# Stationary values and 512-wide weight columns in the experts' second product, and a state-space layer without GpSimd

## The chip, the cores and the metric

The kernel runs on one core of a Trainium2 chip. The metric is the device time of one execution in microseconds; the time before is the median of three runs, 2701.28 us (2698.32 to 2701.37). The engines are TensorE (matmuls; PE, and PEld for its weight loads), VectorE (DVE), ScalarE (ACT), GpSimd (POOL) and SyncE (SP), whose queue issues most loads.

## The reference

A transformer of two parts on 256 positions of width 1024. The first part has a feed-forward layer, a mixer of two attentions, and another feed-forward layer. The second part has two layers. Each is a mixer (a state-space layer first, retention second), then a layer of 16384 experts (PEER), then a gated projection of a side input p. All in float32; the lines that matter here:

```python
seg = jnp.where(causal, cum[:, :, None] - cum[:, None, :], -jnp.inf)   # ssd_chunk_step
w = jnp.exp(seg) * cb[..., None] * dtc[:, None]
y = jnp.einsum('btsgr,bsgrp->btgrp', w, xc)
...
y = y.reshape(B, S, DI).astype(h.dtype) * jax.nn.silu(z)                # ssd_mixer
...
hid = jax.nn.gelu(jnp.einsum('tkd,td->tk', u[ib], xb), approximate=False)   # peer_ffn
return jnp.einsum('tk,tkd->td', (gb * hid).astype(xb.dtype), v[ib])
...
g = jax.nn.sigmoid(rms_norm_2(h, ple_norm[i]) @ ple_gate[i])            # second_block
h = h + g * (p[i] @ ple_proj[i])
```

## The kernel before

The residual x lies feature-major: 8 blocks (d) of 128 features by 256 positions. A float32 product is three matmuls (mm3): both operands are split into a high part (ah, wh) and a rest (al, wl), and the product of the two rests is left out. Weights come through one stream (class Stream) in units of 128 x 1024: SyncE loads w, ScalarE casts it to wh (L252), VectorE subtracts to get wl (L254; with pool_every = 4, as in the state-space layer, GpSimd takes every fourth). Three units are loaded ahead, two or three are split ahead.

The order on each engine is written by the framework's scheduler, which simulates the program with its own costs; code under high_priority is moved forward. Each engine then runs its queue strictly in order.

**Experts (peer).** All 16384 experts are computed for all positions. The first product gives G (two tiles G0 and G1, 64 blocks each), which the gates multiply. In the second product, the loop over e takes 128 units of 128 experts, in pairs; for each of 8 feature blocks d the 128 x 128 weights stand in TensorE and the 256 positions of the values (ah, al) move. The eight sums acc stay in four accumulator banks until the end. At the last pair each d is added to x (L1174) as soon as its sum is complete, and ready(d) calls prep: ScalarE makes ah, VectorE al, ScalarE the square, GpSimd adds the squares into sqa. Two 128-position halves are called t.

**Gated projection (ple).** It loads pT, splits it (ph, pl; L337 and L338), multiplies it with two units (the projection, 48 matmuls of 256 columns, copied to proj) and then multiplies the prepared x with eight units (the gate). The reduction of sqa over features is one matmul (L394). Its tiles lie in memory that the experts' pools have given up.

**State-space layer (ssd).** Per group of 8 heads: conv (cv, three steps of ca, ct) on 6 products, decays (e: cumulative sums plus mask on GpSimd, Exp on ScalarE), core (mt, e times mt, matmuls into po, y), gate (z, tanh, y; squares) and normed. Six of eight heads' e are multiplied on VectorE, two on GpSimd. Products are evacuated by VectorE through four banks. settle rescales x in eight blocks on ScalarE and GpSimd (scale_residual).

Of the kernel before, what the change touches and what calls it, by code (L numbers as in the profile page):

```python
# [21 lines left out]
FT = mybir.dt.float32  # L22
# [4 lines left out]
AF = mybir.ActivationFunctionType  # L27
OP = mybir.AluOpType
# [3 lines left out]
P = 128  # L32
S = 256
NT = S // P
D = 1024
KC = D // P
# [3 lines left out]
NEG = -1e30  # L40
# [4 lines left out]
PK, PH, PT = 128, 8, 16  # L45
# [48 lines left out]
def causal_constants():  # L94


    i = np.arange(P)
    low = np.where(i[None, :] <= i[:, None], 0.0, NEG)
    add = np.concatenate([low, np.zeros((P, P)), low], 1)
    up = np.where(i[None, :] >= i[:, None], 0.0, NEG)  # L100
    top = np.concatenate([up, np.zeros((P, P)), up], 1)
    return add.astype(np.float32), top.astype(np.float32)


# [200 lines left out]
class Program:  # L305
# [120 lines left out]
    def scale_residual(self, g, r, chunks):  # L426
        for c in chunks:
            x = self.x[:, c, :]
            self.nc.scalar.activation(x, x, AF.Identity, scale=self.vec(g, c))
            self.nc.gpsimd.tensor_tensor(x, x, r, OP.mult)  # L430

# [333 lines left out]
    def ssd(self, r, settle, ready):  # L767

        nc, ws = self.nc, self.ws
        with ExitStack() as ctx:  # L770
# [42 lines left out]
            def by_token():  # L813
                ps = self.bank("sc")
                for t in range(NT):
                    for j, k in enumerate((0, 2)):
                        o = (2 * t + j) * H
                        nc.tensor.transpose(ps[:, o:o + H], dt[:, k, t * P:(t + 1) * P], self.ident[:H, :H])
                ps = ps[:, :NT * 2 * H].rearrange("p (t j h) -> p t j h", t=NT, j=2)
                nc.vector.tensor_copy(tok[:, :, 0, :], ps[:, :, 0, :])  # L820
                nc.vector.tensor_scalar(tok[:, :, 1, :], ps[:, :, 1, :], -1.0, None, op0=OP.mult)


            def conv(ps, blk, dst):
# [12 lines left out]

            def decays(g, out):

                for i in range(0, G8, 2):  # L840
                    e = work.tile([P, 2, 384], FT, name="e", bufs=G8 // 2)
                    both = [P, 2, S]
                    nc.gpsimd.tensor_tensor(e[:, :, :S], cums[g][:, i:i + 2, :],
                                            mask[:, None, :S].to_broadcast(both), OP.add)
                    both = [P, 2, P]
                    nc.gpsimd.tensor_tensor(e[:, :, S:], cums[g][:, i:i + 2, P:],
                                            mask[:, None, S:].to_broadcast(both), OP.add)
                    for s in range(2):
                        h = G8 * g + i + s
                        for t, o in ((0, slice(0, S)), (1, slice(S, 384))):  # L850
                            nc.scalar.activation(e[:, s, o], e[:, s, o], AF.Exp, bias=tok[:, t, 1, h:h + 1])
                        out.append(e[:, s, :])
                    yield
                if g + 2 < SSD_G:
                    spread(g + 2)

            def core(g):
# [12 lines left out]
                nc.tensor.matmul(ps[:, :S], bc[:, 0, :P], bc[:, 1, :], start=True, stop=True)  # L870
                nc.tensor.matmul(ps[:, S:384], bc[:, 0, P:], bc[:, 1, P:], start=True, stop=True)
                mt = work.tile([P, 384], FT, name="mt")
                nc.scalar.copy(mt, ps[:, :384])
                yield
                ys[g] = y = work.tile([P, 4, S], FT, name="y")
                for j in range(4):
                    po = self.bank("po")
                    for s in range(2):
                        i = 2 * j + s
                        e = es[i]  # L880
                        (nc.gpsimd if i in (1, 5) else nc.vector).tensor_tensor(e, e, mt, OP.mult)
                        rows, c = slice(64 * s, 64 * s + 64), slice(64 * i, 64 * i + 64)
                        nc.tensor.matmul(po[rows, :S], xd[0][:, c], e[:, :S], start=True, stop=False,
                                         skip_group_check=True)
                        nc.tensor.matmul(po[rows, P:S], xd[1][:, c], e[:, S:], start=False, stop=True,
                                         skip_group_check=True)
                    nc.vector.scalar_tensor_tensor(y[:, j, :], xg[:, j, :], self.vec("ssd_d", 4 * g + j), po[:, :S],
                                                   op0=OP.mult, op1=OP.add)
                    yield

            def gate(ps, g, j):

                last = g == SSD_G - 1
                y = ys[g][:, j, :]
                z, t = work.tile([P, S], FT, name="z", bufs=3), work.tile([P, S], FT, name="zt", bufs=3)
                nc.vector.scalar_tensor_tensor(z, ps[:, :S], 0.5, r(), op0=OP.mult, op1=OP.mult)  # L896
                nc.scalar.activation(t, z, AF.Tanh)
                nc.gpsimd.tensor_tensor(y, y, z, OP.mult)
                nc.vector.scalar_tensor_tensor(y, t, 1.0, y, op0=OP.add, op1=OP.mult)
                self.square(y, j == 0, add=nc.vector if last else nc.gpsimd)  # L900
                if last and j == 2:
                    self.near_sqrt(y[:, 0:1])

            def normed(g):
# [157 lines left out]
    def peer(self, l, r, g, ready):  # L1062
        nc, ws = self.nc, self.ws
        with ExitStack() as ctx:
# [82 lines left out]
                nc.scalar.activation(G[b // (PK // 4)][:, 2 * b % (PK // 2):2 * b % (PK // 2) + 2, :],  # L1147
                                     ps.rearrange("p (a t) -> p a t", a=2), AF.Gelu)
            side.finish()
            acc = self.accumulators()  # L1150
            side = Side(gated(1, work))
            group = []
            for e in range(PK):
# [12 lines left out]
                    continue  # L1166
                if e == PK - 1:
                    self.new_parts()
                for d in (0, 2, 4, 6, 1, 3, 5, 7):
                    k = slice(d * P, (d + 1) * P)  # L1170
                    for i, (wh, wl), h, lo in group:
                        self.mm3(acc[d], wh[:, k], wl[:, k], h, lo, i == 0 and d % 2 == 0, i == PK - 1)
                    if e == PK - 1:
                        nc.vector.scalar_tensor_tensor(self.x[:, d, :], acc[d], 1.0 / GATE, self.x[:, d, :],  # L1174
                                                       op0=OP.mult, op1=OP.add)
                        ready(d)
                group = []
                side.run(1.2)

    def route(self, l, pool, qT, tabs):  # L1180

# [154 lines left out]
        self.ws.lend(stack.enter_context(self.tc.tile_pool(name="spare", bufs=n)), n, until)  # L1336
        return stack

    def accumulators(self):
        self.phase_banks()  # L1340
        four = [self.ps2_pool.tile([P, 2, S], FT, name=f"acc{i}") for i in range(4)]
        return [four[d // 2][:, d % 2, :] for d in range(KC)]

    def run(self):
        nc, tc = self.nc, self.tc
        with ExitStack() as ctx:
# [85 lines left out]
            for l in range(2):  # L1432
                if l == 0:
                    self.phase_banks(sc=2, po=2)
                    self.ws.pool_every = 4
                    self.ssd(r, settle(), before(f"ffn_norm_2{l}"))
                    more.close()
                    spare.close()
                    self.ws.pool_every = 0
                    self.ws.ahead = 2  # L1440
                else:
                    self.phase_banks(sc=1, po=1, pv=2)
                    self.retention(r, before(f"ffn_norm_2{l}"))
                    more.close()
                    spare.close()
# [55 lines left out]
```

## Time and profile before

| | |
|---|---|
| median of three runs | 2701.28 us |
| profiled execution | 2700.06 us |
| its span | 2698.2 us |
| mean granted TensorE clock | 0.991 of full |
| TensorE busy | 2641.6 us, 98% |
| VectorE, ScalarE, GpSimd busy | 2032.9, 1323.9, 313.9 us |

The span is the part of the execution that the trace covers. Matmuls overlap: one of 256 columns is shown 0.28 us long, but the next starts 0.12 us later, so the distance between starts is what counts. Busy time is the union of what an engine runs.

### The profile page before, as it was taken

The page shows a single profiled execution, that of the slowest core. Times are in us where ns is not written, and L with a number is a line of the kernel's source. Part 1 is how long each engine was busy: PE and PEld are TensorE (multiplying, and loading weights), DVE is VectorE, ACT ScalarE, POOL GpSimd, SP SyncE. Part 2 cuts the span into 40 slices and gives each one's busy share as a digit, 9 for nine tenths or more (in the row PEclk, how much of TensorE's full clock was granted, in tenths as well). Part 3 has the DMA queues.
Part 4 walks back from the last instruction along what each step waited for, and adds up shares of the span by engine and source line. Part 5 has one row for each costly group of instructions (what it writes and reads, how often), then busy time and mean ns, then how long its engine had stood idle before and what let it go on. Part 6 is the DMA issues. An engine that isn't in the chain of part 4 may idle for free. (4 is left out here: it accounts for less than half of the span.)

```text
span 2698.2 us, 55170 instructions
## 1 busy us (share of the span) xinstructions
PE 2641.6 (98%) x22838; PEld 2592.4 (96%) x22838; DVE 2032.9 (75%) x3439; ACT 1323.9 (49%) x1810; POOL 313.9 (12%) x303
## 2 busy tenths in 40 slices
PE   8999999988999999999999999999999999999998
PEld 8998899978899999999999999999999999999998
DVE  8656766699779998868875576667999886886556
ACT  6445654666454444343344455555544334434445
POOL 1000100365510220000000020010122000000002
PEclk9999999999999999999999999999999999999999
DMA  6664365553455655555556555555555555556653
GB/s 214 186 186 138 122 191 175 175 185 115 133 177 181 185 171 169 161 174 166 168 182 186 182 172 184 159 171 176 180 187 176 159 163 172 173 163 187 186 181 118
DMA packets 128060, 460.58 MB, mean 171 GB/s; under 512 B 14688, under 2 KB 15424, under 8 KB 127168
## 3 DMA queue, kind: packets, MB, share of 16 engines
q1 hardware_dynamic: 125984, 452.32, 54.0%
q0 software_dynamic: 1536, 4.20, 0.5%
q8 instruction: 179, 2.93, 0.4%
q14 instruction: 73, 0.60, 0.1%
q10 hardware_dynamic: 288, 0.53, 0.1%
HBM read 455.91 MB, written 1.08 MB: 169 GB/s over the span
## 5 line engine op out<-in xcount | busy, mean ns | idle before, releaser
L252 ACT CAST wh<-w 128x1024 fp32r<-128x1024 f32 x856 | 887.1, 1038 | 1207.8 <-PE mm L318 617.4
L254 DVE TENSOR_TENSOR wl<-w,wh 128x1024 fp32r<-128x1024 f32 x842 | 1037.6, 1234 | 457.9 <-ACT wh L252 452.6
L317 PE MATMUL mm<-ah,wh 128*128 128x256 f32 x3448 | 985.6, 286 | 19.9 <-DVE z L896 9.4
L319 PE MATMUL mm<-ah,wl 128*128 128x256 f32 x3448 | 981.6, 285 | 5.7 <-DVE wl L254 5.4
L318 PE MATMUL mm<-al,wh 128*128 128x256 f32 x3448 | 982.3, 285 | 0.1
L317 PEld LDWEIGHTS mm<-ah,wh 128*128 128x128 f32 x3448 | 663.5, 193 | 22.6 <-ACT wh L252 8.4
L319 PEld LDWEIGHTS mm<-ah,wl 128*128 128x128 f32 x3448 | 663.7, 193 | 10.6 <-DVE wl L254 8.8
L318 PEld LDWEIGHTS mm<-al,wh 128*128 128x128 f32 x3448 | 664.0, 193 | 1.1 <-issue 0.5
L317 PE MATMUL acc<-ah,wh 128*128 128x256 f32 x2048 | 580.1, 284 | 0.0
L318 PE MATMUL acc<-al,wh 128*128 128x256 f32 x2048 | 578.8, 283 | 0.0
L319 PE MATMUL acc<-ah,wl 128*128 128x256 f32 x2048 | 575.7, 283 | 0.0
L318 PEld LDWEIGHTS acc<-al,wh 128*128 128x128 f32 x2048 | 393.0, 192 | 0.0
L317 PEld LDWEIGHTS acc<-ah,wh 128*128 128x128 f32 x2048 | 392.5, 192 | 0.0
L319 PEld LDWEIGHTS acc<-ah,wl 128*128 128x128 f32 x2048 | 391.2, 192 | 0.0
L362 POOL TENSOR_TENSOR sqa<-sqa,sqt 128x256 f32<-128x256 f32 x91 | 91.0, 1000 | 1741.9 <-ACT sqt L361 1647.5
L1118 DVE TENSOR_TENSOR G<-mm,G 128x512 f32<-128x512 f32 x128 | 88.1, 689 | 71.7 <-PE mm L1114 71.0
L317 PE MATMUL mm<-hh,wh 128*128 128x256 f32 x352 | 99.0, 281 | 0.0
L318 PE MATMUL mm<-hl,wh 128*128 128x256 f32 x352 | 99.0, 281 | 0.0
L319 PE MATMUL mm<-hh,wl 128*128 128x256 f32 x352 | 99.0, 281 | 0.0
L1102 DVE TENSOR_TENSOR two<-iota,tabs 128x1024 f16<-128x1024 f16 x128 | 87.4, 683 | 0.0
L1114 PE MATMUL mm<-one,two 128*128 128x64 f16 x2048 | 81.9, 193 | 0.0
L338 DVE TENSOR_TENSOR al<-G,ah 128x1024 fp32r<-128x1024 f32 x64 | 78.0, 1218 | 0.7 <-ACT ah L337 0.7
(349 smaller groups left out, 3371.7 us busy)
## 6 DMA issues: line engine op xcount, KB each, us to landing
w<-in_peer_u_dram SPq DMA_DIRECT2D x256, 512.0 KB, 3.6
w<-in_peer_v_dram SPq DMA_DIRECT2D x256, 512.0 KB, 3.6
w<-in_ffn_gu_dram SPq DMA_DIRECT2D x88, 512.0 KB, 3.7
w<-in_ssd_in_dram SPq DMA_DIRECT2D x40, 512.0 KB, 3.6
w<-in_ffn_dn_dram SPq DMA_DIRECT2D x32, 512.0 KB, 3.6
w<-in_peer_q_dram SPq DMA_DIRECT2D x32, 512.0 KB, 3.7
w<-in_ssd_out_dram SPq DMA_DIRECT2D x16, 512.0 KB, 3.6
w<-in_ple_g_dram SPq DMA_DIRECT2D x16, 512.0 KB, 3.6
```

Of the source, the lines that this page charges most:

```text
L252: nc.scalar.copy(h[:, :n], w[:, :n])
L254: (nc.gpsimd if own else nc.vector).tensor_tensor(l[:, :n], w[:, :n], h[:, :n].bitcast(FT), OP.subtract)
L317: mm(ps, h, xh, start=start, stop=False, skip_group_check=True)
L318: mm(ps, h, xl, start=False, stop=False, skip_group_check=True)
L319: mm(ps, l, xh, start=False, stop=stop, skip_group_check=True)
L338: self.nc.vector.tensor_tensor(l, x, h.bitcast(FT), OP.subtract)
L362: (add or nc.gpsimd).tensor_tensor(self.sq[tag], self.sq[tag], t, OP.add)
L1102: nc.vector.tensor_tensor(two, keys.to_broadcast(every), tab[1].to_broadcast(every), OP.is_equal)
L1114: nc.tensor.matmul(ps[:, t, :], two[:, t // 2, :, t % 2], one[i][:, t // 2, :, t % 2], start=i == 0, stop=i == 1)
L1118: nc.vector.tensor_tensor(ga, ps.rearrange("p t e -> p e t"), ga, OP.mult)
```

## The change

Three things change.

1. In the experts' second product the values stand in TensorE (128 positions at a time) and 512 weight columns move. The four sums acc[t][k] are position-major, one bank each. At the end a new function, features, copies each to memory of G0 (ScalarE), transposes it with 16 matmuls per layer, adds the result to x two blocks at a time, and calls ready.
2. The state-space layer has no GpSimd work. The mask becomes a factor (1 or 0) and goes into mt on VectorE; e is exp(-relu(own - other)), all on ScalarE (four Relu and one Exp per pair of heads); e times mt is one VectorE instruction per pair; the gate is three VectorE instructions beside tanh; squares are added on VectorE; scale_residual is one VectorE instruction.
3. All weight subtractions are VectorE's there (pool_every = 0).

```diff
-    up = np.where(i[None, :] >= i[:, None], 0.0, NEG)
-    top = np.concatenate([up, np.zeros((P, P)), up], 1)
+    up = np.where(i[None, :] >= i[:, None], 1.0, 0.0)
+    top = np.concatenate([up, np.ones((P, P)), up], 1)
...
-            self.nc.scalar.activation(x, x, AF.Identity, scale=self.vec(g, c))
-            self.nc.gpsimd.tensor_tensor(x, x, r, OP.mult)
+            self.nc.vector.scalar_tensor_tensor(x, x, self.vec(g, c), r, op0=OP.mult, op1=OP.mult)
...
-                nc.vector.tensor_copy(tok[:, :, 0, :], ps[:, :, 0, :])
-                nc.vector.tensor_scalar(tok[:, :, 1, :], ps[:, :, 1, :], -1.0, None, op0=OP.mult)
+                nc.vector.tensor_copy(tok, ps)
...
             def decays(g, out):
...
                 for i in range(0, G8, 2):
...
-                    both = [P, 2, S]
-                    nc.gpsimd.tensor_tensor(e[:, :, :S], cums[g][:, i:i + 2, :],
-                                            mask[:, None, :S].to_broadcast(both), OP.add)
-                    both = [P, 2, P]
-                    nc.gpsimd.tensor_tensor(e[:, :, S:], cums[g][:, i:i + 2, P:],
-                                            mask[:, None, S:].to_broadcast(both), OP.add)
                     for s in range(2):
...
                         for t, o in ((0, slice(0, S)), (1, slice(S, 384))):
-                            nc.scalar.activation(e[:, s, o], e[:, s, o], AF.Exp, bias=tok[:, t, 1, h:h + 1])
-                        out.append(e[:, s, :])
+                            nc.scalar.activation(e[:, s, o], cums[g][:, i + s, t * P:], AF.Relu, scale=-1.0,
+                                                 bias=tok[:, t, 1, h:h + 1])
+                    nc.scalar.activation(e, e, AF.Exp, scale=-1.0)
+                    out.append(e)
...
-                nc.scalar.copy(mt, ps[:, :384])
+                nc.vector.tensor_tensor(mt, ps[:, :384], mask, OP.mult)
...
                 for j in range(4):
...
+                    e = es[j]
+                    nc.vector.tensor_tensor(e, e, mt[:, None, :].to_broadcast([P, 2, 384]), OP.mult)
                     for s in range(2):
...
-                        e = es[i]
-                        (nc.gpsimd if i in (1, 5) else nc.vector).tensor_tensor(e, e, mt, OP.mult)
...
-                        nc.tensor.matmul(po[rows, :S], xd[0][:, c], e[:, :S], start=True, stop=False,
+                        nc.tensor.matmul(po[rows, :S], xd[0][:, c], e[:, s, :S], start=True, stop=False,
...
-                        nc.tensor.matmul(po[rows, P:S], xd[1][:, c], e[:, S:], start=False, stop=True,
+                        nc.tensor.matmul(po[rows, P:S], xd[1][:, c], e[:, s, S:], start=False, stop=True,
...
             def gate(ps, g, j):
...
-                last = g == SSD_G - 1
...
                 z, t = work.tile([P, S], FT, name="z", bufs=3), work.tile([P, S], FT, name="zt", bufs=3)
...
                 nc.scalar.activation(t, z, AF.Tanh)
-                nc.gpsimd.tensor_tensor(y, y, z, OP.mult)
-                nc.vector.scalar_tensor_tensor(y, t, 1.0, y, op0=OP.add, op1=OP.mult)
-                self.square(y, j == 0, add=nc.vector if last else nc.gpsimd)
-                if last and j == 2:
+                nc.vector.scalar_tensor_tensor(z, t, 1.0, z, op0=OP.add, op1=OP.mult)
+                nc.vector.tensor_tensor(y, y, z, OP.mult)
+                self.square(y, j == 0, add=nc.vector)
+                if g == SSD_G - 1 and j == 2:
...
-            acc = self.accumulators()
+            self.phase_banks()
+            acc = [[self.ps2_pool.tile([P, 512], FT, name=f"acc{t}{k}") for k in range(2)] for t in range(NT)]
...
                 if e == PK - 1:
...
-                for d in (0, 2, 4, 6, 1, 3, 5, 7):
-                    k = slice(d * P, (d + 1) * P)
-                    for i, (wh, wl), h, lo in group:
-                        self.mm3(acc[d], wh[:, k], wl[:, k], h, lo, i == 0 and d % 2 == 0, i == PK - 1)
+                for k in range(2):
+                    w = slice(512 * k, 512 * k + 512)
+                    for t in range(NT):
+                        o = slice(t * P, (t + 1) * P)
+                        for i, (wh, wl), h, lo in group:
+                            self.mm3(acc[t][k], h[:, o], lo[:, o], wh[:, w], wl[:, w], i == 0, i == PK - 1)
                     if e == PK - 1:
-                        nc.vector.scalar_tensor_tensor(self.x[:, d, :], acc[d], 1.0 / GATE, self.x[:, d, :],
-                                                       op0=OP.mult, op1=OP.add)
-                        ready(d)
+                        self.features(acc, k, G[0], ready)
...
+    def features(self, acc, k, room, ready):
+        nc = self.nc
+        with self.tc.high_priority(offset=200):
+            y = [room[:, 4 * k + 2 * t:4 * k + 2 * t + 2, :].rearrange("p a b -> p (a b)") for t in range(NT)]
+            for t in range(NT):
+                nc.scalar.activation(y[t], acc[t][k], AF.Copy, scale=1.0 / GATE)
+            for i in range(0, 4, 2):
+                ps = self.bank().rearrange("p (a t) -> p a t", a=2)
+                for j in range(2):
+                    for t in range(NT):
+                        nc.tensor.transpose(ps[:, j, t * P:(t + 1) * P], y[t][:, (i + j) * P:(i + j + 1) * P], self.ident)
+                d = 4 * k + i
+                nc.vector.tensor_tensor(self.x[:, d:d + 2, :], self.x[:, d:d + 2, :], ps, OP.add)
+                for j in range(2):
+                    ready(d + j)
...
-                    self.ws.pool_every = 4
+                    self.ws.pool_every = 0
```

Where instructions move, engine by engine. First SyncE's queue around the load of pT, first of the two layers; before:

```order
L238 DMA w<-in_ssd_out_dram 128x1024 x16
L238 DMA w<-in_peer_q_dram 128x1024 x16
L238 DMA w<-in_peer_u_dram 128x1024 x128
L238 DMA w<-in_peer_v_dram 128x1024 x62
L1256 DMA pT<-in_pT_dram 128x512
L238 DMA w<-in_peer_v_dram 128x1024 x66
L238 DMA w<-in_ple_p_dram 128x1024 x2
```

after:

```order
L238 DMA w<-in_peer_u_dram 128x1024 x128
L238 DMA w<-in_peer_v_dram 128x1024 x128
L238 DMA w<-in_ple_p_dram 128x1024 x2
L238 DMA w<-in_ple_g_dram 128x1024 x4
L1269 DMA pT<-in_pT_dram 128x512
L238 DMA w<-in_ple_g_dram 128x1024 x4
L238 DMA w<-in_ret_qk_dram 128x1024 x4
```

The load of pT stood behind 62 of the 128 units of the second product; now it stands behind all of them, the projection's two and four of the gate's.

Second, TensorE at the end of the same product (ph, pl: the projection's operand; G: the memory that features borrows); before:

```order
L317 MATMUL acc_14786<-ah,wh 128x256
L318 MATMUL acc_14786<-al,wh 128x256
L319 MATMUL acc_14786<-ah,wl 128x256
L317 MATMUL mm<-ph,wh 128x256
L318 MATMUL mm<-pl,wh 128x256
L319 MATMUL mm<-ph,wl 128x256
L317 MATMUL mm<-ph,wh 128x256
L318 MATMUL mm<-pl,wh 128x256
L319 MATMUL mm<-ph,wl 128x256
L317 MATMUL mm<-ph,wh 128x256
L318 MATMUL mm<-pl,wh 128x256
```

after:

```order
L318 MATMUL acc_14748<-wl,ah 128x512
L319 MATMUL acc_14748<-wh,al 128x512
L317 MATMUL acc_14748<-wh,ah 128x512
L318 MATMUL acc_14748<-wl,ah 128x512
L319 MATMUL acc_14748<-wh,al 128x512
L1187 MATMUL mm<-ident,G_8837 128x128 x16
L317 MATMUL mm<-ph,wh 128x256 x4
L318 MATMUL mm<-pl,wh 128x256
```

The projection's matmuls stood between those of the last pair; now the 16 transposes follow the last product matmul, and the projection follows them. On VectorE, around pl; before:

```order
L254 TENSOR_TENSOR wl<-w,wh 128x1024
L1118 TENSOR_TENSOR G_12053<-mm,G_12053 128x64x8
L254 TENSOR_TENSOR wl<-w,wh 128x1024
L1118 TENSOR_TENSOR G_12053<-mm,G_12053 128x64x8
L338 TENSOR_TENSOR pl<-pT,ph 128x512
L254 TENSOR_TENSOR wl<-w,wh 128x1024 x2
L338 TENSOR_TENSOR al<-G_12053,ah 128x1024
L254 TENSOR_TENSOR wl<-w,wh 128x1024 x5
```

after:

```order
L338 TENSOR_TENSOR al<-G_12012,ah 128x1024
L254 TENSOR_TENSOR wl<-w,wh 128x1024 x8
L1189 TENSOR_TENSOR x<-x,mm 128x512 x4
L254 TENSOR_TENSOR wl<-w,wh 128x1024 x2
L349 SCALAR_TENSOR_TENSOR al<-x,vecs,ah 128x256 x8
L338 TENSOR_TENSOR pl<-pT,ph 128x512
L1280 COPY proj<-mm 128x512 x2
L254 TENSOR_TENSOR wl<-w,wh 128x1024
L1280 COPY proj<-mm 128x512 x2
L254 TENSOR_TENSOR wl<-w,wh 128x1024 x2
```

The subtraction pl stood among the gates' products in the middle of the stage; now it follows the four additions to x, two weight subtractions and eight al of the next stage.

Third, GpSimd in the state-space layer, a piece of its rows before:

```order
L843 TENSOR_TENSOR e<-cums,mask 128x2x256
L846 TENSOR_TENSOR e<-cums,mask 128x2x128
L254 TENSOR_TENSOR wl<-w,wh 128x1024
L843 TENSOR_TENSOR e<-cums,mask 128x2x256
L846 TENSOR_TENSOR e<-cums,mask 128x2x128
L898 TENSOR_TENSOR y<-y,z 128x256
L843 TENSOR_TENSOR e<-cums,mask 128x2x256
L846 TENSOR_TENSOR e<-cums,mask 128x2x128
L898 TENSOR_TENSOR y<-y,z 128x256
L843 TENSOR_TENSOR e<-cums,mask 128x2x256
L846 TENSOR_TENSOR e<-cums,mask 128x2x128
L898 TENSOR_TENSOR y<-y,z 128x256
```

and all that it has between the stages on either side now:

```order
L362 TENSOR_TENSOR sqb<-sqb,sqt 128x256
L362 TENSOR_TENSOR sqa<-sqa,sqt 128x256
L362 TENSOR_TENSOR sqb<-sqb,sqt 128x256
L1205 DMA keys<-in_peer_k_dram 128x256
L362 TENSOR_TENSOR sqa<-sqa,sqt 128x256 x7
L1205 DMA keys<-in_peer_k_dram 128x256 x7
```

None of its rows belongs to the state-space layer any more: the squares of the feed-forward layer before it are followed by the loads and squares of the experts.

## Rows read from the trace of the kernel before

**Rows 1.** The page's head and its part 1 (busy time, share, instructions).
```profile
span 2698.2 us, 55170 instructions
...
PE 2641.6 (98%) x22838; PEld 2592.4 (96%) x22838; DVE 2032.9 (75%) x3439; ACT 1323.9 (49%) x1810; POOL 313.9 (12%) x303
```

**Rows 2.** Busy time by window: stretch, length, busy engines (x), granted clock, DMA share, GB/s.
```profile
1225.00:1300.00 75.00, 75.00 (x765) 74.65 (x763) 62.52 (x92) 30.36 (x30) 0.00 (x0) 1.00 0.55 170
...
1400.00:1550.00 150.00, 150.00 (x1252) 150.00 (x1252) 80.18 (x67) 68.27 (x67) 0.00 (x0) 1.00 0.61 187
...
527.00:722.00 195.00, 168.64 (x1266) 158.39 (x1266) 186.49 (x280) 118.37 (x224) 116.50 (x85) 0.92 0.43 144
```

**Rows 3.** Timeline, TensorE, layer 2: start, length, line; first and last of 19 alike.
```profile
1711.89 0.39 PE L319 MATMUL pv<-wh,bl 128*128 128x512 f32 x1
...
1715.97 0.39 PE L319 MATMUL pv<-wh,bl 128*128 128x512 f32 x1
```

**Rows 4.** Timeline, TensorE, the same product earlier, start of layer 2.
```profile
1621.59 0.63 PE L318 MATMUL pv<-wl,bh 128*128 128x512 f32 x1
...
1624.14 0.63 PE L318 MATMUL pv<-wl,bh 128*128 128x512 f32 x1
```

**Rows 5.** Groups by line, VectorE, 527 to 722 us: count, busy, mean ns, idle before.
```profile
L832 DVE SCALAR_TENSOR_TENSOR ca<-cv,half,ca 128x255 f32<-128x255 f32 (+2 forms) x72 | 52.7, 745 | 0.5 <-ACT ca L830 0.3
...
L254 DVE TENSOR_TENSOR wl<-w,wh 128x1024 fp32r<-128x1024 f32 x33 | 47.5, 1438 | 1.5 <-ACT wh L252 1.4
...
L881 DVE TENSOR_TENSOR e<-e,mt 128x384 f32<-128x384 f32 x24 | 17.0, 764 | 0.4 <-ACT mt L873 0.4
...
L899 DVE SCALAR_TENSOR_TENSOR y<-zt,y 128x256 f32<-128x256 f32 x16 | 14.7, 917 | 0.0
...
L338 DVE TENSOR_TENSOR yl<-y,yh 128x256 fp32r<-128x256 f32 x15 | 11.8, 833 | 0.0
...
L896 DVE SCALAR_TENSOR_TENSOR z<-mm,r 128x256 f32<-128x256 f32 x16 | 6.6, 410 | 0.0
```

**Rows 6.** Timeline of GpSimd, VectorE and TensorE near 575 us: one stall.
```profile
574.62 2.52 POOL L254 TENSOR_TENSOR wl<-w,wh 128x1024 fp32r<-128x1024 f32 x1
...
574.87 3.36 DVE L254 TENSOR_TENSOR wl<-w,wh 128x1024 fp32r<-128x1024 f32 x1
...
578.71 0.55 PE L317 MATMUL mm<-ah,wh 128*128 128x256 f32 x1 [4.35 <-DVE z L896]
```

**Rows 7.** Tiles wl and ca, 527 to 722 us: count, ns min/median/max, first, last start.
```profile
L254 DVE TENSOR_TENSOR wl<-w,wh x33: 1190/1218/3360, 525.6 to 713.5; 128x1024 fp32r<-128x1024 f32 x33
...
L832 DVE SCALAR_TENSOR_TENSOR ca<-cv,half,ca x72: 460/476/2584, 534.4 to 682.3; 128x255 f32<-128x255 f32 x24, 128x254 f32<-128x254 f32 x24, 128x253 f32<-128x253 f32 x24
```

**Rows 8.** Timeline, TensorE: last matmul of layer 1's second product; the scale's reduction.
```profile
1584.15 0.28 PE L319 MATMUL acc<-ah,wl 128*128 128x256 f32 x1
...
1595.44 0.70 PE L394 MATMUL mm<-sqa,ones 128*128 128x256 f32 x2 [0.98 <-POOL sqa L362]
```

**Rows 9.** Tile pT: its two loads, its cast, and time from issue to landing.
```profile
L1256 SPq DMA_DIRECT2D pT<-in_pT_dram x2: 328/328/328, 1378.7 to 2449.5; - x2
...
L337 ACT CAST ph<-pT x2: 620/620/621, 1381.8 to 2452.4; 128x512 fp32r<-128x512 f32 x2
...
DMA to landing us min/median/max: 2.7/2.9/3.0
```

**Rows 10.** Groups by line, ScalarE, 1577 to 1596 us.
```profile
L252 ACT CAST wh<-w 128x1024 fp32r<-128x1024 f32 x7 | 7.3, 1043 | 3.2 <-PE acc L318 1.8 <-DMA w<-in_ple_g_dram 1.0 <-PE mm L318 0.3
...
L348 ACT ACTIVATE ah<-x,vecs 128x256 fp32r<-128x256 f32 x8 | 3.7, 500 | 0.3 <-DVE x L1174 0.3
...
L367 ACT ACT_TABLE_LOAD x1 | 1.3, 1283 | 0.0
```

**Rows 11.** Timeline, GpSimd: first and last of four squares added one after the other.
```profile
1589.28 0.91 POOL L362 TENSOR_TENSOR sqa<-sqa,sqt 128x256 f32<-128x256 f32 x1 [2.35 <-ACT sqt L361]
...
1593.91 1.48 POOL L362 TENSOR_TENSOR sqa<-sqa,sqt 128x256 f32<-128x256 f32 x1 [0.53 <-ACT sqt L361]
```

More of the change, by code (lines that the diff above doesn't have):

```diff
@@ L1337, in lend @@
         return stack
[L1339 to L1342, printed above, removed]
     def run(self):
```

## The prediction

> **What bounds the kernel now.** I read the page's head first: TensorE is busy 2641.6 of 2698.2 us [rows 1], so a saving counts only where it shortens TensorE's own stream or removes one of its few waits. Next the busy time by window [rows 2], to find where those waits are. In the second half of an experts' second product TensorE is busy 150.00 of 150.00 us and starts 1252 matmuls: one every 119.8 ns, at full clock, with VectorE busy 53% and ScalarE 46%. The first half adds the gate matmuls and is as full; VectorE is then at 83%. The state-space stretch, 527 to 722 us, is different: VectorE is busy 186.5 of 195 us, TensorE 168.6, and the granted clock averages 0.92 between its levels of 1.2 and 2.4 GHz. TensorE waits 26 us there, and the clock takes 0.08 x 195 = 16 us more; with neither, its work would need about 153 us. VectorE bounds this stretch. The groups by line [rows 5] say why: its instructions are far longer than their own medians [rows 7]. The timeline shows the way [rows 6]: GpSimd starts a 2.52 us subtraction at 574.62, VectorE's own subtraction beside it takes 3.36 us where the median is 1.22, and TensorE then sits 4.35 us for VectorE's z.
>
> **Part 1, the width.** Removed: 128 experts x 8 blocks x 3 x 2 layers = 6144 matmuls of 256 columns. Added: 128 x 4 x 3 x 2 = 3072 of 512. The trace has the new form already, with the values stationary and 512 weight columns moving, in the second layer's value projection [rows 3]: 18 steps from 1711.89 to 1715.97 us, 226.7 ns each. Two of the old cost 239.6 ns. Saving: 3072 x 12.9 ns = **40 us**, all of it on TensorE, which is what ends both stages. Bounds: nothing, if the spacing stayed at twice the old, and 40. I take 40: the row is the same instruction. What must hold: each weight unit is now used up in 2.72 instead of 2.88 us, and casting it (1.04 us) and subtracting it (1.22 us) stay well under that [rows 7, 10]; the first half brings VectorE from 83% to about 88%.
>
> The Trainium skill (TensorE: Matmul & The Clock Gate, section Back-to-back issue gap) speaks against this size: it gives 262 cycles for 256 columns and 518 for 512, so 6 cycles or 2.5 ns saved per pair, an estimate of 8 us in all instead of 40. The trace does not agree for 256 columns, where it has 119.8 ns and the page 109.
>
> **Part 2, the seam behind the second product.** This costs. Before, the eight sums became ready one after the other, and VectorE, ScalarE and GpSimd prepared the next stage while TensorE still multiplied: from the last product matmul at 1584.15 to the reduction (L394) at 1595.44 there are 11.3 us, 1 of them waiting [rows 8]. 15 of the 48 next projection matmuls (1.8 us) had run earlier, so the seam is 13.1 us of the stream. Now all 16 transposes stand behind the last product matmul, and they read the memory of G0, over which the next stage's pool lies. So the load of pT moves from the middle of the stage (1378.7 us, 200 us early [rows 9]) to behind the last transpose, and everything made from it waits. With T the end of the last product matmul, and no row for a transpose or a 512-column copy out of the accumulator here:
> - The last copy, between 0.50 us (256 columns) and 1.04 us (1024) [rows 10], taken as 0.7, starts about T+0.5, behind a weight cast. Then 8 transposes at about 0.12 us, the spacing of a 256-column matmul (an estimate): T+2.2. Load of pT, 0.3 to issue and 2.9 to land [rows 9]: T+5.3.
> - ScalarE's queue has, ahead of the cast of pT: two weight casts (2.1), eight ah (3.7), two squares (0.8), a table load and one small instruction (1.6) [rows 10]. From T+1.2 these end at T+9.4. So pT has landed, and ScalarE's order decides. Cast 0.62 [rows 9], then VectorE's pl about 0.7: T+10.9.
> - TensorE, in order, has nothing but the projection in front: it idles from T+2.2 to about T+10. Then the rest of the projection (46 x 0.12 = 5.5 us) and 25 matmuls of the gate (3.0 us) to the reduction: T+19.4. The six squares still to be added come 1.54 us apart (three steps from 1589.28 to 1593.91 [rows 11]), from T+10.0 to T+19.3, so they are just hidden.
> - 19.4 against 13.1 is 6 us. After an idle of nearly 8 us I expect the clock at its lower level for a while: the 512-column step was 425 ns once [rows 4], 1.9 times the full rate, for over 2.5 us behind some short waits. I add 2 us.
> That makes 8 us in each layer, **+16 us**. Bounds: 4 (only the load counts) and 14 per layer (ScalarE's queue slips by another 6 us).
>
> **Part 3, the state-space layer without GpSimd.** Off VectorE goes the lengthening, by line [rows 5, 7]: ca 72 x (745 - 476) = 19.4 us; wl 33 x (1438 - 1218) = 7.3; e 24 x (764 - 600, interpolated between 254 and 1024 columns) = 3.9; y 16 x (917 - 410, the length of z) = 8.1; yl 15 x (833 - 410) = 6.3. Sum 45. On VectorE come 10 weight subtractions of GpSimd's in this stretch (43 instead of 33 in its order): 12.2; products of 768 columns, 16 x 0.97 against 24 x 0.60: 1.1; a product more in each of 16 gates: 6.6; 9 additions of squares: 3.7; the mask, 4 x 0.6: 2.4. Sum 26. Of the eight residual scalings seven fall before the stretch, where VectorE has room. Net 19 us less: 186.5 becomes 167.5, still above TensorE's 153, so VectorE remains the bound and the stretch gets shorter by what it loses: **-19 us**. ScalarE gains 16 exponentials of 768 columns (between 0.50 and 1.04 us, 0.85 taken: 13.6) and loses 4 copies (about 2): 118.4 becomes 130 of 176 us, 74%, not a bound on average. Its decays come in batches of up to ten instructions ahead of weight casts, the cover that could go. Bounds: 0 and -42 (195 to 153, TensorE alone).
>
> **Sum.** -40 + 16 - 19 = -43. The profiled execution took 2700.06 us for a span of 2698.2; that gives 2657. The median of the runs, 2701.28, is 1.2 higher: **2658 us**.
>
> **Rivals.**
> 1. The state-space stretch gains nothing: the additions eat the relief, or ScalarE's batches hold casts back. For it: ScalarE's added 12 us, and both engines in order. Against: the stall that goes [rows 6]. -40 + 16: 2677.
> 2. The seams cost 14 us each: -40 + 28 - 19 = -31: 2670. For it: three engines' queues lie on that chain. Against: none is over 9 us long.
> 3. The stretch gets half way from the forecast to its bound, the clock staying at full level: -31 instead of -19, and seams at 5 each: -61: 2640.
> 4. The width saves nothing in this stage: -19 + 16 = -3: 2698. Against: the same instruction measured [rows 3]. The skill's rule above would make that 2690.
> 5. Slower: ScalarE's decays. Each of four groups is 16 Relu (about 0.4 us, since ah takes 0.50 and half of these are half as wide) and 4 exponentials (0.85), 9.8 us in ScalarE's order; if TensorE's weight casts stood behind each group whole, TensorE would wait 39 us in the stretch instead of gaining 19, and with seams at 14 the sum is -40 + 28 + 39 = +27: 2728. It decides from the point where parted weights run out, three units or 8.6 us ahead. Against: casts stand between these instructions in the order.
>
> **Chances.** Forecast 0.49 (its own range 2647 to 2668), rival 1 0.18, 2 0.13, 3 0.11, 4 0.04, 5 0.05. The range for 8 in 10 is 2638 to 2684: it takes in rivals 1, 2 and 3 and leaves out 4 and 5 and the outer parts. A change under 0.2%, 5.4 us, can't be told from none here: faster 0.91 (the forecast and rivals 1 to 3), same 0.04, slower 0.05.
>
> **What would show it.** Right: acc matmuls start 0.227 us apart; TensorE idles 6 to 9 us at the end of both second products, released by ph or pl, with pT issued only then; between the first cv and the last yl VectorE's longest ca is under 0.6 us and the stretch takes about 176 us. Wrong: an acc spacing near 0.24, pl no later than the transposes, or TensorE waiting for wh in the state-space stretch.

## The result and the profile after

The changed kernel takes **2661.06 us** (median of 4 runs, 2659.78 to 2662.18) against 2700.38 (2698.32 to 2701.37) for the kernel before in the same comparison: ratio 0.9855, 95% interval 0.9839 to 0.9871, so 39 us less. Forecast were 2658 us, within 2638 to 2684.

The page's head, as in [rows 1]:

```profile
span 2660.4 us, 49066 instructions
PE 2600.5 (98%) x19798; PEld 2422.3 (91%) x19798; DVE 2005.3 (75%) x3473; ACT 1338.4 (50%) x1824; POOL 191.7 (7%) x216
```

The span falls by 37.8 us, TensorE's busy time by 41.1. The share of 98% is what it was, so it says nothing of where the time came from. For that I cut both spans at the same events of TensorE's timeline: the first and last acc matmul of each layer, and the reduction L394 behind it.

| piece of the span | before, us | after, us | difference |
|---|---|---|---|
| start to first acc of layer 1 (holds the state-space layer) | 1196.8 | 1176.3 | -20.5 |
| first to last acc, layer 1 | 387.4 | 367.3 | -20.0 |
| last acc to L394, layer 1 | 11.3 | 21.7 | +10.5 |
| L394 to first acc of layer 2 | 672.2 | 672.2 | 0.0 |
| first to last acc, layer 2 | 387.4 | 367.4 | -20.0 |
| last acc to L394, layer 2 | 10.6 | 22.9 | +12.3 |
| L394 to the end | 32.6 | 32.5 | -0.2 |

The first acc matmuls of the two layers, before and then after (the number of records, the shortest, median and longest in ns, the first and last start of line L317; lines L318 and L319 follow it):

```profile
L317 PE MATMUL acc<-ah,wh x1024: 280/283/365, 1196.8 to 1583.9; 128*128 128x256 f32 x171
L317 PE MATMUL acc<-ah,wh x1024: 280/283/365, 2267.6 to 2654.7; 128*128 128x256 f32 x171
L317 PE MATMUL acc<-wh,ah x512: 387/389/481, 1176.3 to 1543.2; 128*128 128x512 f32 x171
L317 PE MATMUL acc<-wh,ah x512: 387/389/481, 2237.6 to 2604.6; 128*128 128x512 f32 x171
```

**The width.** Timeline of TensorE in the changed kernel, the last steps of layer 1's product and what follows (start, length, instruction, in brackets the idle time before it and what ended it); these answer to [rows 8]:

```profile
1543.41 0.39 PE L318 MATMUL acc<-wl,ah 128*128 128x512 f32 x1
1543.64 0.39 PE L319 MATMUL acc<-wh,al 128*128 128x512 f32 x1
1543.87 1.99 PE L1187 MATMUL mm<-ident,G 128*128 128x128 f32 x16
1553.92 1.22 PE L317 MATMUL mm<-ph,wh 128*128 128x256 f32 x4 [8.05 <-ACT ph L337]
...
1559.63 0.41 PE L318 MATMUL mm<-pl,wh 128*128 128x256 f32 x1
1559.85 0.31 PE L319 MATMUL mm<-ph,wl 128*128 128x256 f32 x1
...
1565.38 0.59 PE L394 MATMUL mm<-sqa,ones 128*128 128x256 f32 x2
```

The acc matmuls start 0.23 us apart, as those of [rows 3] did. The 16 transposes take 1.99 us together. Then TensorE sits 8.05 us until ScalarE has cast pT into ph; in layer 2 it sits 9.00 us at the same place and 0.66 more for pl. Until 1559.85 the projection's matmuls come 0.213 us apart, then 0.12: behind the idle time the clock runs at its lower level (granted clock 0.50 from 1553.9 to 1559.9 us), and 28 matmuls at 0.093 us more are 2.6 us.

The tile pT, which answers to [rows 9] (two loads, the cast, VectorE's part, landing):

```profile
L1269 SPq DMA_DIRECT2D pT<-in_pT_dram x2: 382/382/383, 1546.1 to 2607.5; - x2
L337 ACT CAST ph<-pT x2: 602/608/614, 1553.3 to 2615.6; 128x512 fp32r<-128x512 f32 x2
L338 DVE TENSOR_TENSOR pl<-pT,ph x2: 676/948/1220, 1553.9 to 2616.8; 128x512 fp32r<-128x512 f32 x2
...
DMA to landing us min/median/max: 3.9/4.1/4.3
```

The load is issued at 1546.1, when the transposes are done, instead of 200 us ahead. It lands by 1550.4 (4.3 us, the longer of the two), but the cast starts at 1553.3. ScalarE's timeline shows what stands ahead of it:

```profile
1545.94 1.99 ACT L252 CAST wh<-w 128x1024 fp32r<-128x1024 f32 x2 [1.01 <-issue]
...
1550.97 1.28 ACT L367 ACT_TABLE_LOAD   x1
1552.27 0.29 ACT L367 ACTIVATE warm<-x,vecs 128x1 f32<-128x1 f32 x1
1552.47 0.89 ACT L348 ACTIVATE ah<-x,vecs 128x256 fp32r<-128x256 f32 x2
1553.26 0.60 ACT L337 CAST ph<-pT 128x512 fp32r<-128x512 f32 x1
```

**The state-space layer.** First cv to last yl runs from 533.4 to 701.8 us, 168 us; before it ran from 531.2 to 722.2, 191 us. VectorE's tile ca and the group of line L254 in that stretch answer to [rows 5, 7]:

```profile
L830 DVE SCALAR_TENSOR_TENSOR ca<-cv,half,ca x72: 446/475/484, 534.7 to 669.2; 128x255 f32<-128x255 f32 x24, 128x254 f32<-128x254 f32 x24, 128x253 f32<-128x253 f32 x24
```
```profile
L254 DVE TENSOR_TENSOR wl<-w,wh 128x1024 fp32r<-128x1024 f32 x45 | 54.6, 1215 | 3.0 <-ACT wh L252 2.9
```

The longest ca falls from 2.58 to 0.48 us, the median stays. The trace of the kernel before shows what a lengthened ca was waiting for. All 31 of the 72 that took over 0.55 us end 0.28 us (277 to 284 ns) after an instruction of GpSimd ends; one such pair:

```profile
577.11 2.25 POOL L843 TENSOR_TENSOR e<-cums,mask 128x512 f32<-128x512 f32 x1
578.87 0.76 DVE L832 SCALAR_TENSOR_TENSOR ca<-cv,half,ca 128x254 f32<-128x254 f32 x1
```

The ten lengthened wl end 1.08 us after one, as the pair in [rows 6] does. Two more lines were lengthened in the kernel before (same window as [rows 5]); they now take 415 and 417 ns:

```profile
L836 DVE SCALAR_TENSOR_TENSOR xg<-ct,ca 128x256 f32<-128x256 f32 x16 | 10.6, 665 | 0.4 <-ACT ct L835 0.4
...
L836 DVE SCALAR_TENSOR_TENSOR bc<-ct,ca 128x256 f32<-128x256 f32 x8 | 6.5, 807 | 0.0
```

VectorE takes all weight subtractions now, 45 instead of 33, at a mean of 1.22 instead of 1.44 us. By window, as in [rows 2] (stretch, length, busy time and count of TensorE, its weight loads, VectorE, ScalarE, GpSimd, then the granted clock):

```profile
523.00:702.00 179.00, 161.67 (x1295) 154.07 (x1294) 164.56 (x322) 131.69 (x241) 0.00 (x0) 0.95 0.47 157
```

VectorE is still the busiest engine there, 92% against TensorE's 90%, and the longest waits of TensorE are for it: 10.7 us in five waits for cv, 3.6 us in one for y.

### The profile page after: what moved, and what is told of

Same layout as the page of the kernel before. It is cut to its first block, busy times and chain, and to the rows that moved or that the text cites. A ratio compares the mean times of both kernels' runs of the same rounds, so it can differ in the third digit from the quotient of the medians.

```text
span 2660.4 us, 49066 instructions
## 1 busy us (share of the span) xinstructions
PE 2600.5 (98%) x19798; PEld 2422.3 (91%) x19798; DVE 2005.3 (75%) x3473; ACT 1338.4 (50%) x1824; POOL 191.7 (7%) x216
## 3 DMA queue, kind: packets, MB, share of 16 engines
HBM read 455.91 MB, written 1.08 MB: 172 GB/s over the span
## 4 chain that ended last, share of the span: by engine, by line
PE 89%; DVE 6%; ACT 2%; issue 1%; POOL 0%; DMA 0%; POOLq 0%; DVEq 0%; ACTq 0%
PE mm L317 19%; PE mm L318 18%; PE mm L319 18%; PE acc L317 9%; PE acc L318 9%; PE acc L319 9%; PE mm L1108 2%; DVE wl L254 2%; DVE eq L1238 1%; DVE f L1241 1%; PE pv L318 1%; PE pv L319 1%; PE sc L1208 1%; PE pv L317 1%; ACT wh L252 0%
## 5 line engine op out<-in xcount | busy, mean ns | idle before, releaser
L254 DVE TENSOR_TENSOR wl<-w,wh 128x1024 fp32r<-128x1024 f32 x856 | 1045.4, 1223 | 394.2 <-ACT wh L252 391.7
L317 PE MATMUL mm<-ah,wh 128*128 128x256 f32 x3448 | 985.5, 286 | 18.8 <-DVE cv L826 10.7
L319 PE MATMUL mm<-ah,wl 128*128 128x256 f32 x3448 | 980.0, 285 | 5.6 <-DVE wl L254 5.4
L318 PE MATMUL mm<-al,wh 128*128 128x256 f32 x3448 | 982.0, 285 | 0.0
L317 PEld LDWEIGHTS mm<-ah,wh 128*128 128x128 f32 x3448 | 662.8, 192 | 22.0 <-ACT wh L252 8.6
L319 PEld LDWEIGHTS mm<-ah,wl 128*128 128x128 f32 x3448 | 662.6, 192 | 9.3 <-DVE wl L254 8.5
L318 PEld LDWEIGHTS mm<-al,wh 128*128 128x128 f32 x3448 | 663.4, 192 | 0.8 <-issue 0.3
L318 PE MATMUL acc<-wl,ah 128*128 128x512 f32 x1024 | 400.5, 391 | 0.0
L319 PE MATMUL acc<-wh,al 128*128 128x512 f32 x1024 | 399.3, 391 | 0.0
L317 PE MATMUL acc<-wh,ah 128*128 128x512 f32 x1024 | 361.3, 392 | 0.0
L319 PEld LDWEIGHTS acc<-wh,al 128*128 128x128 f32 x1024 | 192.1, 188 | 38.9
L317 PEld LDWEIGHTS acc<-wh,ah 128*128 128x128 f32 x1024 | 192.1, 188 | 38.9
L318 PEld LDWEIGHTS acc<-wl,ah 128*128 128x128 f32 x1024 | 192.5, 188 | 38.1
L362 POOL TENSOR_TENSOR sqa<-sqa,sqt 128x256 f32<-128x256 f32 x82 | 81.8, 997 | 1157.1 <-ACT sqt L361 1027.6
L337 ACT CAST ah<-G 128x1024 fp32r<-128x1024 f32 x64 | 67.5, 1054 | 85.6 <-PE acc L318 84.5
L317 PE MATMUL mm<-hh,wh 128*128 128x256 f32 x352 | 99.0, 281 | 0.0
L318 PE MATMUL mm<-hl,wh 128*128 128x256 f32 x352 | 99.0, 281 | 0.0
L319 PE MATMUL mm<-hh,wl 128*128 128x256 f32 x352 | 99.0, 281 | 0.0
L1108 PEld LDWEIGHTS <-two 128*128 128x128 f16 x2048 | 69.5, 97 | 21.7 <-issue 16.5
```

The lines of the kernel that those rows point to most:

```text
L254: (nc.gpsimd if own else nc.vector).tensor_tensor(l[:, :n], w[:, :n], h[:, :n].bitcast(FT), OP.subtract)
L317: mm(ps, h, xh, start=start, stop=False, skip_group_check=True)
L318: mm(ps, h, xl, start=False, stop=False, skip_group_check=True)
L319: mm(ps, l, xh, start=False, stop=stop, skip_group_check=True)
L337: self.nc.scalar.copy(h, x)
L362: (add or nc.gpsimd).tensor_tensor(self.sq[tag], self.sq[tag], t, OP.add)
```

## The experiments

The theory: 40 us from the width, some 20 from GpSimd's silence in the state-space layer, some 20 given back because pT's memory lies under the transposes' source. All kernels are variants of the changed one unless said; the kernel before took 2698.98 us in the first four comparisons (15 runs) and 2699.75 in the last three (9 runs).

**1 and 2. Each part alone.** The kernel before with the new `peer` and `features`, and the changed kernel with the old `peer`:

```diff
 width_only: before, with after's peer() and features()
 ssd_only:   after, with before's peer()
```

> The kernel before with only the second product changed (128 stationary columns of values, 512 moving weight columns, transposes and the new layout behind them); the state-space layer is that of before. Theory: the three parts of the gain lie one behind the other on TensorE's path and add up. The two products give 20 us each back (1024 x 3 matmuls, 226.7 instead of 239.6 ns) and the two stretches behind them cost 10.4 and 12.3 us, so 2700 - 40 + 23 = 2683 us, between 2679 and 2687. Rival: the changed kernel's first stretch of 20 us less is not the state-space layer's alone but comes in part from the new product (its other memory plan and order of loads); then this kernel gains more than 25 us, under 2675.

> The changed kernel with the second product of before (256 moving columns): only the state-space layer is new. Theory: it gives the 20 us of the stretch up to the first product and nothing else, 2680 us, between 2677 and 2683. Rival: the state-space layer's instructions save less by themselves, 2685 to 2695.

Measured: 2678.39 us (ratio 0.9923, 0.9908 to 0.9938) and 2679.08 us (0.9927, 0.9912 to 0.9942): 20.6 and 19.9 us less. The sum, 40.5, is the whole change's 39 within what these intervals tell. The first lies 0.6 us below its range, the second within. In width_only the first acc starts at 1194.8 us, so the stretch before it is that of the kernel before but for 2 us, and TensorE's 8.1 us for ph are there; in ssd_only the longest ca is 0.49 us. Within these intervals the parts add up, and both rivals fall.

**3. Another room for the sums.** One word:

```diff
-                        self.features(acc, k, G[0], ready)
+                        self.features(acc, k, G[1], ready)
```

> The changed kernel with one word changed: the sums of the second product are copied into the memory of the second gate tile (G1) instead of the first (G0). Theory: the stretch behind the product is long because the next stage's input pT lies over G0, so its load waits for the transposes, and ScalarE then casts it behind its own preparation (TensorE waits 8.05 and 9.00 us for that cast). With G1 pT can be loaded half a product earlier, the projection's 48 matmuls stand directly behind the 16 transposes, and each stretch falls from 21.7 and 22.9 to some 13 to 15 us: 2661 - 14 to 17 = 2644 to 2647 us, and TensorE's wait for the cast is gone. Rival A: the copies, transposes and the preparation of the eight columns that follow set the end by themselves, and the wait moves to the gate matmuls (for ah): 2655 to 2661. Rival B: the earlier load of pT stands in the way of the weights' loads: 2661 or more.

Measured: **2651.36 us** (0.9825, 0.9812 to 0.9839), some 10 us less than the changed kernel, and the fastest of all. The load of pT now starts at 1355.3 us, and TensorE's timeline behind layer 1's product is:

```profile
1543.37 1.25 PE L1187 MATMUL mm<-ident,G 128*128 128x128 f32 x10
1545.86 0.87 PE L1187 MATMUL mm<-ident,G 128*128 128x128 f32 x6 [1.24 <-ACT G L1182]
1546.48 0.37 PE L317 MATMUL mm<-ph,wh 128*128 128x256 f32 x1
...
1560.61 0.70 PE L394 MATMUL mm<-sqa,ones 128*128 128x256 f32 x2 [2.37 <-POOL sqa L362]
```

The wait of 8.05 us is gone and so is the slow clock (0.12 us steps from 1546.7 on, granted clock 1.00): G0's memory was the cause of both. But I had expected 14 to 17 us. Three smaller waits came up in its place: 1.24 us for the last copy out of the accumulator, 2.37 for GpSimd's sums of squares, which the idle time had hidden, and 2.6 for a part of the next columns (bl) after L394. Theory and rival A each had a share: the distance to L394 falls from 21.7 to 17.5 us, not to 13 to 15 (18.2 from 22.9 in layer 2).

**4. The same sums on VectorE.** On top of 3, the squares behind the product go into two buffers and VectorE adds them:

```diff
-                    self.prep(d, g)
+                    self.prep(d, g, squares=add is None)
+                    if add:
+                        self.square(self.x[:, d, :], d == 0, add=add, two=True)
...
-                self.peer(l, r, f"ffn_norm_2{l}", before(f"ple_norm_2{l}", 6))
+                self.peer(l, r, f"ffn_norm_2{l}", before(f"ple_norm_2{l}", 6, nc.vector))
```

> The kernel with G1 as room, and the squares of the column preparation behind the second product summed by VectorE (with two buffers) instead of GpSimd. Theory: with pT early, what ends last in the stretch is GpSimd's chain of sums: the reduction at L394 waits 2.37 and 2.60 us for it, each step of the chain taking some 1.25 us from square to square. On VectorE a sum takes 0.42 us, so the two waits go: 2651 - 5 = 2646 us, between 2644 and 2648. Rival: VectorE, busy 14.7 of the 20 us there, is then late with the parts of the columns and of the weights that TensorE wants next, and the wait only changes its name: 2650 to 2655.

Measured: 2656.39 us (0.9840, 0.9826 to 0.9853), 5 us more than 3 instead of 5 less. My theory fell, and the rival (2650 to 2655) had the sign but not the mechanism. TensorE:

```profile
1565.52 1.19 PE L394 MATMUL mm<-sqa,ones 128*128 128x256 f32 x2 [4.99 <-DVE sqa L362]
```

and ScalarE just before it:

```profile
1556.46 0.41 ACT L361 ACTIVATE sqt<-x 128x256 f32<-128x256 f32 x1
1560.21 1.99 ACT L252 CAST wh<-w 128x1024 fp32r<-128x1024 f32 x2 [3.33 <-PE mm L318]
1562.11 0.41 ACT L361 ACTIVATE sqt<-x 128x256 f32<-128x256 f32 x1
```

VectorE's sums take 0.42 us. The last three squares, though, now stand behind two weight casts in ScalarE's order, and those wait 3.33 us for TensorE to free a buffer. With GpSimd as the adder these casts came after the squares. The program order changed with the engine, and the order cost more than the engine gave.

**5. GpSimd busy, for nobody.** Work on a private tile, waited for by no one, issued at the start of the state-space layer:

```diff
+            def busy(n):
+                nc.gpsimd.tensor_tensor(idle[:, 0, :n], idle[:, 1, :n], idle[:, 2, :n], OP.mult)
...
                     out.append(e)
+                    busy(512)
+                    busy(256)
...
                     e = es[j]
+                    busy(384)
...
                 self.square(y, j == 0, add=nc.vector)
+                busy(256)
+                busy(256)
```

> The changed kernel with work for GpSimd that nothing reads and that waits for nothing: 64 multiplications of SBUF operands in the state-space layer (16 of 512, 16 of 384 and 32 of 256 columns, some 98 us at the durations of the kernel before, 1.82, 1.20 and 1.05 us), issued back to back. Theory: the gain of the state-space layer comes from GpSimd's silence, since VectorE's instructions with two operands in SBUF last until GpSimd's instruction beside them ends; before, 121 us of GpSimd's work cost VectorE some 45 us, so 98 us cost some 36 us of VectorE's time, of which part lies beside TensorE's full stretches: 15 to 30 us more, 2676 to 2691, and the longest ca rises from 0.48 to over 1.5 us while those of the PSUM-reading cv stay. Rival: the gain comes from fewer and differently cut instructions and from waits that went with GpSimd's place in the chain, and work beside it that nothing waits for costs nothing: within 2 us of 2661.

Measured: 2698.01 us (0.9994, 0.9985 to 1.0004): 37 us more than the changed kernel where 15 to 30 were expected, and 32 in span (the profiled execution, 2693.79 us, is among the shortest of ten). That is more than all of the state-space layer's gain. The edit issues 80 multiplications and not 64, since decays adds 16 of 256 columns; they took 96.3 us of GpSimd, from 518 to 622 us. VectorE's line of ca in 522 to 622 us, and from there on:

```profile
L836 DVE SCALAR_TENSOR_TENSOR ca<-cv,half,ca x30: 460/943/1550, 544.4 to 615.5; 128x255 f32<-128x255 f32 x10, 128x254 f32<-128x254 f32 x10, 128x253 f32<-128x253 f32 x10
...
L836 DVE SCALAR_TENSOR_TENSOR ca<-cv,half,ca x42: 467/472/482, 623.9 to 707.5; 128x255 f32<-128x255 f32 x14, 128x254 f32<-128x254 f32 x14, 128x253 f32<-128x253 f32 x14
```

The median doubles while GpSimd works and is back at once when it ends. All 26 ca over 0.55 us again end 0.27 to 0.28 us after an instruction of GpSimd. The same 100 us by window, pool_scratch and then the changed kernel:

```profile
522.00:622.00 100.00, 65.82 (x465) 61.23 (x463) 95.71 (x105) 52.75 (x94) 93.96 (x79) 0.81 0.36 125
```
```profile
522.00:622.00 100.00, 91.56 (x738) 88.56 (x738) 92.49 (x175) 75.45 (x134) 0.00 (x0) 0.97 0.52 178
```

VectorE is as busy in both, but gets 105 instructions done instead of 175, and TensorE 465 matmuls instead of 738, at a lower clock. Busy time doesn't tell a stretched engine from a working one; the count does. The cv, which has one operand in PSUM, stays at 402 to 420 ns throughout. The Trainium skill (GPSIMD Engine Reference, section Specifications) says that GpSimd contends with VectorE's instructions with two SBUF inputs; the trace agrees, and adds the price. No data passes from GpSimd here, so waits on its results are excluded as the price. But the added work also changed the scheduler's order: from 522 us on VectorE and ScalarE run their instructions of this layer in another order than in the changed kernel, so this comparison alone can't give the 37 us to GpSimd.

**6. A third of it.** Only the gate's 32 multiplications of 256 columns, 31.6 us of GpSimd's time (the edit against experiment 5):

```diff
                     out.append(e)
-                    busy(512)
-                    busy(256)
...
                     e = es[j]
-                    busy(384)
```

> pool_scratch with half its instructions, the 32 multiplications of 256 columns alone: some 34 us of GpSimd's time at the start of the state-space layer instead of 101 us. Theory: the price follows the time in which GpSimd runs beside a full VectorE, 32 us of span for 101 us: some 11 us, 2668 to 2676. Rival: it is the first collision that costs (a wait that shifts the whole stretch), and the price stays near pool_scratch's: over 2685; or a layout effect of the scratch memory, the same for any amount.

Measured: 2667.22 us (0.9879, 0.9864 to 0.9894): 6 us more than the changed kernel, 1 us below the range and about half of the 11 us in proportion. Only 6 of the 72 ca are lengthened, against 26. VectorE, ScalarE and the queues that issue loads have the same order here as in experiment 5, and the scratch memory is the same. So the 31 us between the two are the price of the 48 further multiplications, 65 us of GpSimd's time. Neither a first collision nor order or memory can make them; in the 6 us the new order and the 32 multiplications can't be told apart.

**7. Similar work where VectorE has time.** 64 multiplications (16 of 512, 16 of 384 and 32 of 256 columns, 87.8 us of GpSimd), in the second half of layer 1's second product:

```diff
                     gates.close()
+                    if l == 0:
+                        slack = ctx.enter_context(self.tc.tile_pool(name="slack", bufs=1))
+                        idle = slack.tile([P, 512], FT, name="idle")
+                        nc.gpsimd.memset(idle, 1.0)
+                        for n in 16 * (512, 256, 384, 256):
+                            nc.gpsimd.tensor_tensor(idle[:, :n], idle[:, :n], idle[:, :n], OP.mult)
```

> The changed kernel with the same 64 GpSimd multiplications as in pool_scratch (some 97 us, read by nobody), but in the second half of the first second product, where TensorE is full and VectorE busy about half the time (4.9 of 10 us in the window 2590:2600). Theory: VectorE's two-SBUF-input instructions are stretched there too (the longest wl from 1.3 us to over 2 us), but it has the time, and the weights' ring covers a late wl: within 3 us of 2661. Rival: GpSimd's work costs time wherever it runs (by holding more than VectorE's operands, such as ScalarE's or the transfers): 10 us or more.

Measured: 2661.40 us (0.9861, 0.9846 to 0.9876), no change. The order on the other engines is that of the changed kernel. By window, this kernel and then the changed one:

```profile
1361.00:1454.00 93.00, 93.00 (x412) 77.01 (x411) 69.85 (x45) 45.48 (x45) 87.90 (x65) 1.00 0.63 194
```
```profile
1361.00:1454.00 93.00, 93.00 (x411) 76.99 (x411) 53.87 (x46) 45.40 (x44) 0.00 (x0) 1.00 0.62 197
```

VectorE is stretched here too, 16 us more for the same instructions (the group of wl below, here and then in the changed kernel), ScalarE and the transfers are not, and TensorE does not notice.

```profile
L254 DVE TENSOR_TENSOR wl<-w,wh 128x1024 fp32r<-128x1024 f32 x35 | 55.8, 1612 | 16.0 <-ACT wh L252 15.9
L254 DVE TENSOR_TENSOR wl<-w,wh 128x1024 fp32r<-128x1024 f32 x35 | 42.7, 1223 | 30.0 <-ACT wh L252 29.9
```

VectorE's instructions are stretched in both places; the price came only where VectorE was the bound.

## Why the prediction came out right

- **Width, -40: right.** The two products give 40.0 us between their first and last acc. Since 15 projection matmuls (1.8 us per layer) moved out of each product, 36.4 of it are the width's own, 3.2 under the 39.6 worked out from [rows 3]. The trace has most of these 3 us where the gates' small matmuls break into the first half: the acc step after such a break takes 0.32 us instead of 0.23 (37 steps per layer), and took 0.20 instead of 0.12 (25 steps), which is 1.2 us less gain per layer. Rival 4 falls: the row of the product itself is as fast as that of [rows 3]. With it falls the estimate of 8 us from the figures in the Trainium skill (TensorE: Matmul & The Clock Gate, section Back-to-back issue gap), which gives them for single matmuls and not for a stream.
- **Seams, +16: the mechanism right, the size 3 us short.** The ledger has +10.5 and +12.3; less the 1.8 us each that moved, +8.7 and +10.5, 19 in all. Step by step in layer 1, with T = 1544.0 us: transposes end at T+1.8 (T+2.2 forecast), pT is issued at T+2.1 and lands by T+6.4 (T+5.3), the cast starts at T+9.2 (T+9.4), so ScalarE's order decides as said, TensorE idles 8.05 us, and L394 comes at T+21.3 (T+21.4). The lower clock cost 2.6 us where I took 2. Most of the excess is layer 2's: its waits are 9.00 and 0.66 us. Experiment 3 shows that the memory of G0 makes the long waits, and that without them 10 of the 19 us remain. The sums of squares were hidden, as forecast, but not just: they came 1.25 us apart instead of 1.54 and ended at T+17.4 instead of T+19.3, 3.9 us before L394. They are part of why experiment 3 gave 10 us and not 15: with the first wait gone they were next in line.
- **State-space layer, -19: the mechanism right, 20.5 measured, the closeness in part luck.** The lengthening of VectorE's instructions goes as a whole (ca to its median), experiments 5 to 7 show that GpSimd's mere activity makes it, and VectorE stays the bound (its busy time falls by 21.9 us, 186.5 to 164.6). How much of the 20.5 us is GpSimd's silence and how much the new cut of the instructions was not measured apart. The stretch from cv to yl falls to 168 us and not 176: of the forecast's window of 195 us these events span 191, and 23 came off instead of 19, but 2 of them by a later start. The residual scalings that moved to VectorE ahead of it were costed at nothing, but took 3.3 us, and TensorE waits 5.1 us for the first cv instead of 1.7. The sum also left out xg and bc, 7.1 us of lengthening, and counted ten of GpSimd's subtractions where twelve moved (2.4 us). These three errors nearly cancel. Of the casts that rival 5 feared, TensorE's matmuls show no wait for wh in the stretch, and its weight loads 1.5 us.
- **Sum.** In span, -36.4 + 19.2 - 20.5 - 0.2 is the -37.8 measured, but for rounding; -43 were forecast. The width gave 3.6 us too little, the seams cost 3.2 too much, and the state-space layer gave 1.5 more. Rivals 1 and 5 fall with the 20.5 us there, rival 3 too, which wanted 31, and rival 2's 14 us per seam is above the 8.7 and 10.5 measured.

## What to carry to other kernels

An engine that seems off the path can set the speed of another: before giving GpSimd a share, look at the maximum beside the median of VectorE's instructions with two operands in SBUF, and count instructions per window, not busy time. Scratch space in memory that the next stage's pool will reuse makes that stage's first load wait for the last reader; pick room that is not under it. When a wait is removed, read the next one in the same timeline before sizing the gain, and when work changes engines, read the order of every queue it touches.

## What was not expected of the hardware

- Each lengthened ca (31 of 72 before, 26 in experiment 5) ends 0.27 to 0.28 us after an instruction of GpSimd ends, each lengthened wl 1.08 us after one: VectorE's instruction waited for GpSimd's, and the profile shows the wait as busy time.
- 65 us more of GpSimd's work, with VectorE and ScalarE in the same order, cost 31 us (experiment 5 against 6), beside a VectorE shown 96% busy. 88 us of similar work cost nothing beside one busy 58% without it.
- In experiment 7 a wl under GpSimd's work took 1612 ns in the mean against 1223, while ScalarE's busy time over the same 93 us was 45.5 against 45.4 us.
